# One diffusion layer with mixer and two FFNs: the beginning of the first FFN, the modulation passes beside the mixer and the joint to the second FFN reordered

## Chip, cores and metric

The kernel runs on one core of a Trainium2 chip. The metric is the device time of one launch in microseconds, the median of several runs. Five engines work beside each other, each through its own queue in order: TensorE (PE; its weight loads are shown as PEld), VectorE (DVE), ScalarE (ACT), GpSimd (POOL) and SyncE (SP), which here issues most DMAs.

## The reference

One layer of a diffusion backbone in fp32, batch 1, 256 latent tokens x and 256 context tokens ctx, width D = 2048:

```python
mod_l = (silu(c) @ w_mod + b_mod).reshape(9, D)        # shift, scale, gate of three sub-layers; mod_c likewise
def half_step_ffn(x, mod, i, g, w_up, w_down):
    h = rms_norm(x, g) * (1 + mod[i + 1]) + mod[i]
    a, b = split(h @ w_up, 2)
    return x + 0.5 * mod[i + 2] * ((silu(a) * b) @ w_down)
xl, xc = half_step_ffn(x, mod_l, 0, ...), half_step_ffn(ctx, mod_c, 0, ...)
# mixer: one projection w_in of both sequences; 8 heads of GQA with RoPE over context and latents,
# 8 heads of a bidirectional mLSTM (depthwise convolution of 5 taps and SiLU on its q and k); then w_out
xl = xl + mod_l[5] * mixer(xl, xc)
xl = half_step_ffn(xl, mod_l, 6, ...)
return rms_norm(xl, g_final)
```

`w_mod` alone is 2048 x 18432 numbers, 151 MB. It is read while other work runs.

## The kernel before

**Precision.** Every operand of a large product is split into a high and a low part in fp32r: `split` (L110) lets ScalarE copy a loaded weight to `hi` (L118) and VectorE subtract to get `lo` (L119). A product is three matmuls into the same PSUM bank, `mm3` (L138 to L142): high by high, one mixed product, the other mixed product. Operands named `hhi` and `hlo` are those of the normalised, scaled and shifted tokens.

**Order of the work.** Instructions are written in program order and a scheduler may move them, except where `tc.keep_in_program_order` pins them. `Pinned` (L70) wraps an engine so that every instruction issued through it is pinned; in the first stage VectorE and TensorE are wrapped (L84), ScalarE isn't. Their instructions all appear as L78 in the trace. Where work of two kinds is to run side by side, Python generators are advanced in turn: `steps` runs one forward some steps, `weave` advances a second one after each step of a first, `drain` runs one to its end.

**The beginning of FFN1** (L449 to L604). SP loads the conditions cc, the four token tiles xs (context 0 and 1, latents 0 and 1, 1 MB each, L510), the small vectors vecs (L511), then units of 1 MB of w_mod, tile `mraw`, into four buffers (L530). `diagonal` (L465) multiplies the conditions with an identity on VectorE, and `spread` (L473) broadcasts them over the 128 partitions by eight fp32 matmuls, copied out to cB by VectorE (context) and ScalarE (latents). `x_tile` (L483) takes the squares of a token tile (ScalarE, L153; half of the last tile's on VectorE), its factor, and scales all its columns. The 16 column groups of 128 are then taken in `BLOCKS` (L36): (0,1), (1,2), then seven of two. For a block, `mod_sums` (L533) multiplies the condition with modulation units on TensorE (`tr<-mraw,cP`), one unit of a two-group block goes to VectorE instead (two passes of 128x2048 over `mraw` and cB, "still", L579), `mod_turned` transposes the rows, the tokens are transposed (`x_turned`, `to_hT`), `affine_split` (L377) applies scale and shift and splits into hhi and hlo, and `products` (L403) multiplies with six groups of w_up1, which it loads as strided pieces (L415). The products of a block are stepped between the modulation units of the next one.

**FFN1** (to L1104) keeps TensorE busy with sums of weights that DMAs accumulate; the change doesn't touch it.

**The mixer** (L1135 to L1718) runs its projections in turn. Beside them, `Beside` (L264) computes modulation rows for the second FFN: 96 passes of 128x1024 on VectorE (`mod_half`, L198, with the pair `sr`, `early` or `late` as its buffer), each over 512 KB of w_mod loaded a few passes ahead into the tiles listed at L1165 (after pass 50 three of them end, after pass `N_MIXER` = 80 two more, so that only sr0 is left until three "late" tiles come at L1632). A list of points (pass, step) at L1167 says before which step of the mixer a pass may be issued; steps are advanced by `next(beside["part"])`, at each loaded weight tile. The mLSTM's queries come from the loop at L1412: for each head four columns of matmuls, a convolution on VectorE (L1287), SiLU on ScalarE (L1420), and mqT (L1422); `latents` (L1345), stepped inside that loop, issues the scores (L1355) of a finished head. Attention (softmax at L1536 to L1559) is followed by `out_proj` (L1656): for four column blocks first the groups (2, 0, 3) of w_out, then, in a second loop (L1710), the last group (1,), with the residual.

**The joint to FFN2** (L1699 to L1764). The residual is transposed (`x2_transposed`), the rest of `beside` drained (L1720), the norm's factor computed and broadcast (`rr`, L1727, rB, L1729). Then the pool of FFN2 opens, `scaled` (L1742) applies the scale, and for four quarters q `products` runs on w_up2, with `scaled` of the next quarter woven in and the exact form `h2` (L1751) after it. The fourth group of the first up-projection is done at L1794 to L1805 (`sab`), and `token_forms` (L1840) begins the sums of tokens with `difference` (L1850) for the rest of FFN2.

Of the kernel before, what the change touches and what calls it, by code (L numbers as in the profile page):

```python
# [32 lines left out]

PACE2 = 70 / 73

# [14 lines left out]
def tile_layer(ctx: ExitStack, tc: tile.TileContext, I: dict, out: bass.AP):  # L50
# [33 lines left out]
    vector, tensor = [nc.vector], [nc.tensor]  # L84
# [25 lines left out]
    def split(raw, n=2048):  # L110
# [3 lines left out]
        for h in range(2):  # L114
            hi = wp.tile([P, 1024], F32R, tag="hi", name="hi", bufs=4)[:, :half]
            lo = wp.tile([P, 1024], F32R, tag="lo", name="lo", bufs=4)[:, :half]
            src = raw[:, h * half : (h + 1) * half]
            nc.scalar.activation(hi, src, AF.Copy)  # L118
            vector[0].tensor_tensor(lo, src, hi.bitcast(F32), op=ALU.subtract)  # L119
            parts.append((hi, lo))  # L120
# [30 lines left out]
    def sumsq(dst, x, n=512):  # L151
        junk = sm.tile([P, 512], BF16, tag="junk", name="junk", bufs=1)
        nc.scalar.activation(junk[:, :n], x, AF.Square, accum_out=dst)  # L153
# [223 lines left out]
    def affine_split(src, n, pairs, hh, hl):  # L377

        h = scratch[-1].tile([P, 2, 256], F32, tag="h", name="h", bufs=2)
        for kk, (k, s) in enumerate(pairs):  # L380
            sc, sh = SC[:, n, s, k : k + 1], SH[:, n, s, k : k + 1]
            nc.scalar.activation(hh[:, kk, :], src[:, kk, :], AF.Identity, scale=sc, bias=sh)
            if kk:
                vector[0].tensor_scalar(h[:, kk, :], src[:, kk, :], sc, sh, op0=ALU.mult, op1=ALU.add)
            else:
                nc.scalar.activation(h[:, kk, :], src[:, kk, :], AF.Identity, scale=sc, bias=sh)
# [16 lines left out]
    def products(wup, pre, k0, k1, hhi, hlo, early=False):  # L403
# [7 lines left out]
        def load(u0):  # L411
            nu = min(most, 2 * NPRE - u0)
            raw = raw_tile(n * nu)
            tc.keep_in_program_order(
                nc.sync.dma_start(  # L415
                    raw.rearrange("p (u c) -> p u c", u=nu),
                    wup[u0 // 2 : (u0 + nu) // 2, :, :, k0 * P : k1 * P].rearrange("f a p c -> p (f a) c"),
                )
            )
            return raw, nu  # L420

        ahead = load(0)
        if early:
            wt = split(ahead[0], n * ahead[1])
        yield
        for u0 in range(0, 2 * NPRE, most):
            raw, nu = ahead
            if u0 or not early:
                wt = split(raw, n * nu)
            if u0 + most < 2 * NPRE:  # L430
                ahead = load(u0 + most)
            for u in range(nu):
                b = pre[(u0 + u) // 2][u % 2]
                for k in range(k0, k1):
                    w = slice(u * n + (k - k0) * P, u * n + (k - k0 + 1) * P)
                    mm3(b, *wt(w), hhi[:, k, :], hlo[:, k, :], k == 0, k == KT - 1)
# [13 lines left out]
    with pool(name="st", bufs=1) as st:  # L450
# [12 lines left out]
        junk = st.tile([P, 1024], BF16, name="junkv")  # L463

        def diagonal(s):  # L465
            m = raw_tile()[:32]
            m3 = m.rearrange("p (k c) -> p k c", k=KT)
            vector[0].tensor_tensor(
                m3, cc.unsqueeze(1).to_broadcast([32, KT, P]), ident[:32, s * KT : (s + 1) * KT].unsqueeze(2).to_broadcast([32, KT, P]), op=ALU.mult
            )  # L470
            return m

        def spread(s, m):  # L473
            for q in range(4):
                b = pre[q // 2][q % 2]
                w = slice(q * CB, (q + 1) * CB)
                tensor[0].matmul(b, ones[:32, :], m[:, w], start=True, stop=True)
                if s:
                    nc.scalar.activation(cB[:, s, w], b, AF.Copy)
                else:  # L480
                    vector[0].tensor_copy(cB[:, s, w], b)

        def x_tile(s, t, shared=False):  # L483

            x = xs0[s, t]
            ss4 = sm.tile([P, 4], F32, tag="ss4", name="ss4", bufs=4)
            for cb in range(NCB):
                if not (shared and cb % 2):
                    sumsq(ss4[:, cb : cb + 1], x[:, cb * CB : (cb + 1) * CB])
                else:  # L490
                    xc = x[:, cb * CB : (cb + 1) * CB]
                    vector[0].scalar_tensor_tensor(junk[:, :CB], xc, 1.0, xc, op0=ALU.mult, op1=ALU.mult, accum_out=ss4[:, cb : cb + 1])
            s1 = sm.tile([P, 1], F32, tag="s1", name="s1")
            vector[0].tensor_reduce(s1, ss4, axis=AX.X, op=ALU.add)
            r = rsqrt_mean(s1, D)
            for c in (slice(0, 256), slice(256, D)):
                vector[0].tensor_scalar(x[:, c], x[:, c], r, None, op0=ALU.mult)
# [9 lines left out]
        for s in (CTX, LAT):  # L507
            for t in range(2):
                x = xs0[s, t] = st.tile([P, D], F32, name=f"xs{s}{t}")
                tc.keep_in_program_order(nc.sync.dma_start(x, xsrc[s][t * P : (t + 1) * P, :]))  # L510
        tc.keep_in_program_order(nc.sync.dma_start(vecs, I["vecs"]))  # L511
        diagonals = [diagonal(s) for s in (CTX, LAT)]
        spread(CTX, diagonals[0])
        x_tile(CTX, 0)
        x_turned(0, CTX, 0)
        spread(LAT, diagonals[1])
        for s, t in ((CTX, 1), (LAT, 0), (LAT, 1)):
            x_tile(s, t, s == LAT and t == 1)
            x_turned(0, s, t)

# [4 lines left out]
        prods = iter(())  # L525
        unit = iter(range(32))

        def mod_unit():
            raw = st.tile([P, 2048], F32, tag="mraw", name="mraw", bufs=4)
# [3 lines left out]
        def mod_sums(i, k0, k1, last=iter(())):  # L533
# [16 lines left out]
            nc.scalar.activation(row, b, AF.Copy)  # L550
# [18 lines left out]
        for k0, k1 in BLOCKS:  # L569
            kk = slice(k0, k1)  # L570
            following = products(I["w_up1"], pre, k0, k1, hhi, hlo, k0 == 0)
            if k1 - k0 == 2:
                raw = mod_unit()
            for i in range(2):
                for _ in mod_sums(i, k0 if i else k1 - 1, k1, following if i else iter(())):
                    steps(prods, 3 - (k1 - k0))
                if k0 == 0:
                    mod_turned()
# [10 lines left out]
            if k1 - k0 == 1:  # L589
                tb = tbank() if k0 else first_tb  # L590
                if k0:
                    for s in (CTX, LAT):
                        for t in range(2):
                            x_turned(k0, s, t, tb)
# [5 lines left out]
            prods = following  # L600
            if k1 == KT:
# [43 lines left out]
    with pool(name="f1u", bufs=1) as f1u:  # L645
# [26 lines left out]
        for f in range(NPRE, FB):  # L672
            pab = []
            for ab in range(2):
                wt = load_split(I["w_up1"][f, ab])
# [459 lines left out]
    with ExitStack() as mx:  # L1135
        m1 = mx.enter_context(pool(name="m1", bufs=2))
# [22 lines left out]
        mm = mx.enter_context(pool(name="mm", bufs=1))  # L1159
        mm2cm = pool(name="mm2", bufs=1)  # L1160
        mm2 = mm2cm.__enter__()
        N_EARLY, N_MIXER = 50, 80
# [4 lines left out]
        mods = Beside(mm, 5, 8, tiles, ((6, 12), (N_EARLY, 54), (62, 90), (72, 126), (N_MIXER, 162), (96, 176)))  # L1167
# [244 lines left out]
        for h in range(NH):  # L1412
            b = bank()[:, :T]
            for n, _ in enumerate(channels("w_mq", h, T, b)):
                if (h, n) in ((0, 3), (1, 2)):
                    steps(st)
                if n % 2:
                    steps(lat)
# [279 lines left out]

        def x2_transposed(cb):  # L1699
            for k0 in (4 * cb, 4 * cb + 2):  # L1700
                tb = tbank()
                for kk in range(2):
                    for t in range(2):
                        k = k0 + kk
                        nc.tensor.transpose(tb[:, kk * 256 + t * P : kk * 256 + (t + 1) * P], x2[t][:, k * P : (k + 1) * P], ident)
                nc.scalar.activation(x2T[:, k0 : k0 + 2, :], tb.rearrange("p (k c) -> p k c", k=2), AF.Copy)
                yield

        xT = iter(())
        for cb in range(NCB):  # L1710
# [501 lines left out]
```

## Time and profile before

| | us |
|---|---|
| median of 3 runs | 2664.96 |
| lowest, highest | 2663.31, 2666.14 |
| profiled execution | 2667.12 |
| its span in the trace | 2665.4 |
| mean granted TensorE clock | 0.995 |

The profile is one execution, recorded instruction by instruction. Its page gives the busy time of each engine; its views give busy time by stretches (with the granted TensorE clock, 1.00 being full speed), groups of instructions by line, operation and tile, the waits of an engine by what ended them, and a timeline. A row of the timeline has start, duration, engine, line, operation, output and inputs, shape and count, and in brackets how long the engine sat idle before it and what released it. Lines are those of the kernel before; a helper's line (L78, L118, L119, L198) stands for all its callers.

### The profile page before, as it was taken

Reading aid. Unit: us, or ns where it says so; the run is one execution under the profiler, and the core shown is the slowest. Engines: PE = TensorE matmul, PEld = TensorE weight load, DVE = VectorE, ACT = ScalarE, POOL = GpSimd, SP = SyncE. Lnnn points to the kernel's source line nnn. Section 1 sums busy time; section 2 is a strip of 40 time slices with the busy share of each in tenths; the row PEclk is TensorE's granted clock in tenths of the full one; section 3 lists DMA queues with packets and bytes.
Section 4 is the critical chain, followed back from the end, with each engine's and each line's share of the span. In section 5 each row is a group of like instructions: output and inputs, shape, how many; then the busy total and the mean of one; then the engine's idle time right before and its main releaser. Section 6 shows DMA issues by size and latency. Waiting matters only on the chain. (4 is left out here: it accounts for less than half of the span.)

```text
span 2665.4 us, 33742 instructions
## 1 busy us (share of the span) xinstructions
PE 2609.3 (98%) x12718; PEld 2160.6 (81%) x12718; DVE 2118.4 (79%) x2838; ACT 1367.3 (51%) x1748; POOL 211.1 (8%) x271
## 2 busy tenths in 40 slices
PE   8999999999999999999999999998999999999998
PEld 4688887888888878888879889876898888888886
DVE  5797878878888788888886878688698777777867
ACT  4354444544444555444454347454476655555554
POOL 0000001100000100010111000120000000000001
PEclk9999999999999999999999999999999999999999
DMA  9979999999999988889986865567579898989975
GB/s 345 353 211 270 265 277 267 259 275 278 261 282 264 273 229 237 223 207 233 228 236 221 308 226 201 174 221 254 193 253 292 285 291 290 290 274 283 279 228 170
DMA packets 135027, 679.97 MB, mean 255 GB/s; under 512 B 14152, under 2 KB 23624, under 8 KB 73552
## 3 DMA queue, kind: packets, MB, share of 16 engines
q1 hardware_dynamic: 107504, 500.59, 51.1%
q0 software_dynamic: 27360, 177.22, 34.0%
q8 instruction: 100, 1.64, 0.2%
q14 instruction: 63, 0.52, 0.1%
HBM read 659.87 MB, written 17.89 MB: 254 GB/s over the span
## 5 line engine op out<-in xcount | busy, mean ns | idle before, releaser
L118 ACT ACTIVATE hi<-raw 128x1024 fp32r<-128x1024 f32 (+3 forms) x542 | 560.5, 1038 | 613.7 <-PE mm L142 467.6
L119 DVE TENSOR_TENSOR lo<-raw,hi 128x1024 fp32r<-128x1024 f32 (+1 forms) x524 | 630.5, 1209 | 277.1 <-ACT hi L118 259.2
L118 ACT ACTIVATE hi<-chain 128x1024 fp32r<-128x1024 f32 x320 | 337.8, 1059 | 262.4 <-PE mm L142 133.0
L119 DVE TENSOR_TENSOR lo<-chain,hi 128x1024 fp32r<-128x1024 f32 x320 | 387.1, 1222 | 93.6 <-ACT hi L118 91.0
L140 PE MATMUL mm<-hi,hhi 128*128 128x512 f32 (+3 forms) x1024 | 394.6, 386 | 6.9 <-DVE c L747 6.9
L142 PE MATMUL mm<-hi,hlo 128*128 128x512 f32 (+3 forms) x1024 | 387.6, 379 | 0.0
L141 PE MATMUL mm<-lo,hhi 128*128 128x512 f32 (+3 forms) x1024 | 387.4, 378 | 0.1
L198 DVE SCALAR_TENSOR_TENSOR junk<-sraw,cBh 128x1024 fp8e5<-128x1024 f32 x192 | 234.4, 1221 | 29.9 <-DMA sraw<-in_w_mt 27.6
L140 PEld LDWEIGHTS mm<-hi,hhi 128*128 128x128 f32 x1024 | 192.7, 188 | 39.4 <-ACT hi L118 8.6
L142 PEld LDWEIGHTS mm<-hi,hlo 128*128 128x128 f32 x1024 | 192.7, 188 | 33.6
L141 PEld LDWEIGHTS mm<-lo,hhi 128*128 128x128 f32 x1024 | 193.0, 188 | 31.1 <-DVE lo L119 0.3
L142 PE MATMUL mm<-hi,hid2l 128*128 128x512 f32 x352 | 137.6, 391 | 0.0
L140 PE MATMUL mm<-hi,hid2h 128*128 128x512 f32 x352 | 137.4, 390 | 0.0
L141 PE MATMUL mm<-lo,hid2h 128*128 128x512 f32 x352 | 137.3, 390 | 0.0
L140 PE MATMUL mm<-hi,h2hi 128*128 128x512 f32 x320 | 125.2, 391 | 1.5 <-DVE sab L1804 1.5
L141 PE MATMUL mm<-lo,h2hi 128*128 128x512 f32 x320 | 124.8, 390 | 0.0
L142 PE MATMUL mm<-hi,h2lo 128*128 128x512 f32 x320 | 124.8, 390 | 0.0
L644 POOL DMA_DIRECT2D chain<-in_w_up1b x60 | 53.0, 883 | 740.8 <-DVE lo L119 576.2
L140 PE MATMUL mm<-hhi,hi 128*128 128x512 f32 (+1 forms) x288 | 101.9, 354 | 0.0
L142 PE MATMUL mm<-hhi,lo 128*128 128x512 f32 (+1 forms) x288 | 99.5, 345 | 0.0
L141 PE MATMUL mm<-hlo,hi 128*128 128x512 f32 (+1 forms) x288 | 99.2, 345 | 0.0
L198 DVE SCALAR_TENSOR_TENSOR sr<-sr,cBl 128x1024 f32<-128x1024 f32 x66 | 81.0, 1235 | 13.4 <-DMA sr<-in_w_mt 13.2
(477 smaller groups left out, 5515.7 us busy)
## 6 DMA issues: line engine op xcount, KB each, us to landing
raw<-in_w_dn SPq DMA_DIRECT2D x70, 1024.0 KB, 7.3
sraw<-in_w_mt SPq DMA_DIRECT2D x128, 512.0 KB, 7.4
chain<-in_w_up1b POOLq DMA_DIRECT2D x60, 1024.0 KB, 10.9
raw<-in_w_up2b SPq DMA_DIRECT2D x50, 1024.0 KB, 6.9
raw<-in_w_up1b SPq DMA_DIRECT2D x40, 1024.0 KB, 8.5
mraw<-in_w_m SPq DMA_DIRECT2D x32, 1024.0 KB, 7.3
sr<-in_w_mt SPq DMA_DIRECT2D x63, 512.0 KB, 5.4
chain<-in_w_dn POOLq DMA_DIRECT2D x30, 1024.0 KB, 8.4
```

The lines of the kernel that those rows point to most:

```text
L118: nc.scalar.activation(hi, src, AF.Copy)
L119: vector[0].tensor_tensor(lo, src, hi.bitcast(F32), op=ALU.subtract)
L140: tensor[0].matmul(out_ap, sh, mh, start=first, stop=False, skip_group_check=skip)
L141: tensor[0].matmul(out_ap, sh, ml, start=False, stop=False, skip_group_check=skip)
L142: tensor[0].matmul(out_ap, sl, mh, start=False, stop=last, skip_group_check=skip)
L198: ins = nc.vector.scalar_tensor_tensor(junk() if junk else raw, raw, 1.0, cB[s], op0=ALU.mult, op1=ALU.mult, accum_out=mT[:, i, s, kt, h : ...
L644: accum = lambda dst, src: nc.gpsimd.dma_start(dst, src, accum_op=ALU.add)
```

## The change

Nothing of what is computed is left out. Six parts:

1. *Beginning of FFN1.* The conditions are split into fp32r high and low parts and spread by sixteen fp32r matmuls with eight VectorE products of 32x1024 ahead of them; all copies to cB are ScalarE's. vecs and two modulation units are loaded before the token tiles. Block 0's modulation sums and rows are issued before the tokens' scaling. The squares of a tile (two quarters on ScalarE, two on VectorE) are issued before the scaling of the tile ahead of it, only its first 256 columns are scaled at once, and the rest is scaled later (`others`). ScalarE is pinned as well until block (2, 4) is done.
2. *`affine_split`*: ScalarE makes both high parts first, then h of the first half; VectorE h of the second.
3. *`products`*: the weights come from new inputs `w_pre1`, `w_pre2`, laid out so that each load is contiguous. For each unit all matmuls with hhi come first, those with hlo last. A second load may be issued ahead (`both`).
4. *Mixer*: the list of points has 23 entries instead of 6, `N_MIXER` is 85 instead of 80, and one step of `latents`, at (h, n) = (1, 1), is left out of the loop.
5. *Joint to FFN2*: FFN2's pools open before the second loop of `out_proj`, the rest of `beside` is drained before that loop, `scaled` is woven into it, the loads and first step of the first quarter's `products` are issued before the last residual, the last transposes are woven into that quarter, and the factor is computed after it.
6. *Fourth group*: the first subtraction of `difference` is issued after the gate's product.

The core of the diff:

```diff
-        N_EARLY, N_MIXER = 50, 80
-        mods = Beside(mm, 5, 8, tiles, ((6, 12), (N_EARLY, 54), (62, 90), (72, 126), (N_MIXER, 162), (96, 176)))
+        mods = Beside(mm, 5, 8, tiles, PACE)
+PACE = (4, 2), (12, 13), (19, 19), (26, 28), (33, 37), (37, 44), (42, 51), (48, 54), (52, 61), (55, 70), (58, 76), (59, 85), (63, 96)
+PACE += (70, 102), (72, 109), (75, 118), (76, 130), (77, 144), (80, 152), (83, 163), (85, 166), (86, 174), (96, 181)
+        N_EARLY, N_MIXER = 50, 85
...
-            if kk:
-                vector[0].tensor_scalar(h[:, kk, :], src[:, kk, :], sc, sh, op0=ALU.mult, op1=ALU.add)
-            else:
-                nc.scalar.activation(h[:, kk, :], src[:, kk, :], AF.Identity, scale=sc, bias=sh)
+        for kk, (sc, sh) in enumerate(cols):
+            scalar[0].activation(hh[:, kk, :], src[:, kk, :], AF.Identity, scale=sc, bias=sh)
+        scalar[0].activation(h[:, 0, :], src[:, 0, :], AF.Identity, scale=cols[0][0], bias=cols[0][1])
+        vector[0].tensor_scalar(h[:, 1, :], src[:, 1, :], *cols[1], op0=ALU.mult, op1=ALU.add)
...
-                for k in range(k0, k1):
-                    mm3(b, *wt(w), hhi[:, k, :], hlo[:, k, :], k == 0, k == KT - 1)
+                for k, (wh, wl) in ws:
+                    tensor[0].matmul(b, wh, hhi[:, k, :], start=k == 0, stop=False)
+                    tensor[0].matmul(b, wl, hhi[:, k, :], start=False, stop=False)
+                for k, (wh, wl) in ws:
+                    tensor[0].matmul(b, wh, hlo[:, k, :], start=False, stop=k == KT - 1)
...
+        def squares(s, t):
+            ss4 = sm.tile([P, 4], F32, tag="ss4", name="ss4", bufs=4)
+            for cb in range(NCB):
+                xc = xs0[s, t][:, cb * CB : (cb + 1) * CB]
+                if cb >= 2:
+                    vector[0].scalar_tensor_tensor(junk[:, :CB], xc, 1.0, xc, op0=ALU.mult, op1=ALU.mult, accum_out=ss4[:, cb : cb + 1])
+                else:
+                    sumsq(ss4[:, cb : cb + 1], xc)
+            return ss4
...
+        tc.keep_in_program_order(nc.sync.dma_start(vecs, I["vecs"]))
+        ready += [mod_unit(), mod_unit()]
+        for s in (CTX, LAT):
+            for t in range(2):
+                x = xs0[s, t] = st.tile([P, D], F32, name=f"xs{s}{t}")
+                tc.keep_in_program_order(nc.sync.dma_start(x, xsrc[s][t * P : (t + 1) * P, :]))
+        prods = products(1, pre, 0, 1, hhi, hlo, True)
+        scalar[0] = Pinned(nc.scalar)
+        for copy in spread(CTX, diagonals(CTX)):
+            copy()
+        drain(mod_sums(0, 0, 1))
+        drain(mod_sums(1, 0, 1))
+        ms = diagonals(LAT)
+        ss = squares(CTX, 0)
+        mod_turned()
...
+        copies = spread(LAT, ms)
+        r = factor(ss)
+        for n, (s, t) in enumerate(((CTX, 1), (LAT, 0), (LAT, 1))):
+            ss = squares(s, t)
+            if n < 2:
+                copies[2 * n]()
+                copies[2 * n + 1]()
+            first_columns(*divmod(n, 2), r)
+            r = factor(ss)
+        steps(prods)
+        first_columns(LAT, 1, r)
+        x_scaled(0, first_tb)
+        others(2)
...
-                if n % 2:
+                if n % 2 and (h, n) != (1, 1):
                     steps(lat)
...
+        drain(beside["part"])
+        mmcm.__exit__(None, None, None)
+        m1cm.__exit__(None, None, None)
...
             weave(out_proj(cb, (1,), bs), xT)
+            if cb == NCB - 1:
+                pre = [[bank()[:, : T + 2], bank()[:, : T + 2]] for _ in range(NPRE)]
+                prods = products(2, pre, 0, 4, h2hi, h2lo, both=True)
+                steps(prods)
             residual(cb, bs)
...
-            xT = x2_transposed(cb)
-        drain(xT)
-        drain(beside["part"])
+            xT = chain(scaled(cb - 1), x2_transposed(cb)) if cb else x2_transposed(cb)
...
+            if not q:
+                weave(prods, xT)
+                drain(xT)
+                factor()
+            else:
+                weave(prods, scaled(3) if q == 2 else iter(()))
             drain(h2(q))
...
-            nc.vector.tensor_tensor(sa, sa, pab[1], op=ALU.mult)
+            gated = nc.vector.tensor_tensor(sa, sa, pab[1], op=ALU.mult)
...
-                sub(v, h1, h2)
+                with tc.issue_after(gated.ins):
+                    sub(v, h1, h2)
```

222 lines of the change are left out of this document (116 added, 106 removed).

## The prediction

> **What bounds the kernel now.** I read the page first, then the busy time by stretches, then TensorE's waits. The page's first row (engine, busy time, share, instructions):
>
> ```profile
> PE 2609.3 (98%) x12718; PEld 2160.6 (81%) x12718; DVE 2118.4 (79%) x2838; ACT 1367.3 (51%) x1748; POOL 211.1 (8%) x271
> ```
>
> TensorE is busy 2609.3 of 2665.4 us. The change removes no product of weight, so a gain can come only from the 56 us in which TensorE idles, and from stretches in which its clock was halved. Where are they? Busy time by stretches (columns: PE, PEld, DVE, ACT, POOL busy, granted TensorE clock, DMA share, GB/s):
>
> ```profile
> 32.10:40.00 7.90, 7.39 (x52) 5.18 (x53) 1.93 (x8) 1.18 (x4) 0.00 (x0) 1.00 0.94 340
> 40.00:132.20 92.20, 87.98 (x747) 58.97 (x745) 65.78 (x118) 35.16 (x68) 0.00 (x0) 1.00 0.96 355
> ...
> 140.00:500.00 360.00, 356.24 (x1601) 294.32 (x1600) 303.30 (x363) 174.75 (x200) 30.11 (x34) 1.00 0.94 262
> ...
> 1600.00:1620.00 20.00, 16.39 (x105) 15.22 (x104) 14.51 (x29) 11.16 (x20) 0.76 (x2) 0.83 0.52 182
> 1830.00:1870.00 40.00, 32.51 (x148) 24.03 (x147) 36.29 (x69) 16.36 (x28) 1.36 (x2) 0.91 0.68 235
> 1870.00:1910.00 40.00, 40.00 (x197) 33.42 (x196) 27.06 (x40) 17.68 (x23) 0.00 (x0) 1.00 0.50 168
> ```
>
> The FFN itself (140 to 500) and the output projection (1870 to 1910) leave TensorE idle 1% or less. Two stretches of the mixer stand out. In 1600 to 1620 it idles 3.6 us, and the clock of 0.83 costs another 20 x 0.17 = 3.4 us. In 1830 to 1870 it idles 7.5 us, and 0.91 costs 40 x 0.09 = 3.6. What it waited for (us in total, times, longest):
>
> ```profile
> PE mm L1355 <- DVE mqT L1422: 3.6, 1, 3.6
> PE tr L1550 <- DVE pr L1544: 3.6, 1, 3.6
> ...
> PE mm L78 <- DVE hlo L78: 2.6, 4, 0.8
> ...
> PE mm L78 <- DVE lo L78: 2.0, 7, 0.4
> ...
> PE mm L140 <- DVE sab L1804: 1.5, 1, 1.5
> ...
> PE tr L78 <- DMA mraw<-in_w_m: 1.0, 3, 0.4
> ...
> PE tr L1728 <- DVE rr L1727: 0.8, 1, 0.8
> ```
>
> Nearly all these end on VectorE: TensorE is the bound, and its gaps are places where VectorE's order in program brings one small result late. I take the change in four terms.
>
> **1. The beginning.** The first product of FFN1 starts at 32.07 (start, duration, engine, line, operation):
>
> ```profile
> 29.84 1.94 PE L78 MATMUL tr<-mraw,cP 128*32 128x128 f32 x32
> 32.07 0.80 PE L78 MATMUL mm<-hhi,hi 128*128 128x512 f32 x1 [0.29 <-ACT hhi L382]
> ...
> 39.75 0.60 PE L78 MATMUL tr<-ident,xs 128*128 128x128 f32 x4
> ```
>
> Ahead of it lie these (groups of the first 32 us: busy us, mean ns):
>
> ```profile
> L153 ACT ACTIVATE junk<-xs 128x512 bf16<-128x512 f32 x14 | 8.8, 629 | 3.6 <-DMA xs<-in_ctx 3.2
> ...
> L78 DVE TENSOR_TENSOR raw<-cc,ident 32x2048 f32<-32x2048 f32 x2 | 4.5, 2271 | 0.0
> ...
> L479 ACT ACTIVATE cB<-mm 128x512 f32<-128x512 f32 x4 | 2.4, 597 | 3.9 <-PE mm L78 3.9
> ...
> L382 ACT ACTIVATE hhi<-mm,SH,SC 128x256 fp32r<-128x256 f32 x2 | 1.1, 564 | 1.2 <-DVE SC L78 1.2
> ```
>
> and the loads (the bandwidth in 40 slices of the first 30 us, and the token squares, whose first instruction starts when the first 1 MB tile has landed):
>
> ```profile
> GB/s 0 0 21 175 284 426 415 404 426 415 448 404 437 415 459 404 448 393 415 459 368 310 380 395 448 415 437 404 437 297 369 438 437 371 98 0 109 175 437 393
> ...
> L153 ACT ACTIVATE junk<-xs x14: 629/629/630, 6.1 to 15.9; 128x512 bf16<-128x512 f32 x14
> ```
>
> At 426 GB/s, 1 MB takes 2.46 us, so data flow from about 6.1 - 2.5 = 3.6. SP's queue now issues cc, vecs, two modulation units, the four token tiles, the first weights, then modulation again. Two units and vecs push every token tile back by 2 x 2.46 + 0.35 (vecs has 144 KB) = 5.3 us: ctx lands at 11.4 and 13.8, x at 16.3 and 18.7, the first 384 KB of weights at 19.7. In exchange block 0's modulation rows, which came behind the tiles before, are done while x is still landing.
>
> The spread of the conditions becomes eight VectorE products of 32x1024, about half of 2271 ns each, 9.1 us instead of 4.5; it starts near 3.8 and ends near 13, under the loads. Its fp32r matmuls are not in this trace: between the 0.4 us of a 128x512 product here and the fp32 ones that they replace; I take the former, and either end is hidden under the landing of x. ScalarE's queue is now in program order: the squares of x's first tile at 16.3 (two of 0.63 plus 0.12 of read-out, 1.5), two cB copies (1.2), the squares of the second (1.5): 20.5. Sum, rsqrt, 256 columns and the transpose take about 2.2 more with their handovers, the split 2 x 0.56, and one modulation unit of 1.94 stands ahead of the first product in TensorE's order. That gives 25.8; with the weights' splits (0.5 each) in ScalarE's queue in between I take 26.7, **5.4 us earlier**. What is deferred (1792 columns of each tile, 1.15 each by half of the difference of such rows) goes behind the first split, in VectorE's slack (65.78 of 92.20).
>
> Then the pitch of the blocks. The scaling's new order and the products' new order meet here:
>
> ```profile
> 92.00 0.56 ACT L386 ACTIVATE h<-tr,SH,SC 128x256 f32<-128x256 f32 x1
> ...
> 92.44 1.02 ACT L382 ACTIVATE hhi<-tr,SH,SC 128x256 fp32r<-128x256 f32 x2
> ...
> 93.04 0.55 DVE L78 TENSOR_SCALAR h<-tr,SC,SH 128x256 f32<-128x256 f32 x1 [2.65 <-ACT hhi L382]
> ...
> 96.61 0.50 PE L78 MATMUL mm<-hhi,lo 128*128 128x512 f32 x1 [0.27 <-DVE lo L78]
> ```
>
> VectorE's h waited for ScalarE's second hhi; with both hhi first it can start 0.45 earlier, and hlo and lo behind it. But hlo is asked for last now and lo second, one matmul of 0.23 sooner than before, and lo comes behind hlo on VectorE, so the hlo wait of 2.6 does not vanish: it turns into a lo wait. Net 0.22 a block, 1.5 over seven; the mraw waits (1.0) should shrink, since the units are loaded ahead. The relaid weights load in fewer, longer pieces, but no row shows TensorE waiting for them: nothing. Term: 5.4 + 1.5 + 0.3 = **7**, bounds 3.5 (half of the earlier start) and 10 (all waits of the blocks gone).
>
> **2. The first mLSTM scores** wait for mqT:
>
> ```profile
> 1600.90 1.22 DVE L198 SCALAR_TENSOR_TENSOR sr<-sr,cBl 128x1024 f32<-128x1024 f32 x1
> ...
> 1602.05 1.22 DVE L198 SCALAR_TENSOR_TENSOR sr<-sr,cBl 128x1024 f32<-128x1024 f32 x1
> ...
> 1605.89 1.22 DVE L119 TENSOR_TENSOR lo<-raw,hi 128x1024 fp32r<-128x1024 f32 x1 [0.18 <-ACT hi L118]
> ...
> 1608.05 0.29 DVE L1422 TENSOR_SCALAR mqT<-cy 128x256 f32<-128x256 f32 x1 [0.15 <-ACT cy L1420]
> ...
> 1608.49 2.05 PE L1355 MATMUL mm<-mqT,mkT 128*128 128x256 f32 x4 [3.61 <-DVE mqT L1422]
> ```
>
> In the changed order one pass instead of two stands ahead of this convolution on VectorE (1.15 of pitch), and one weight split fewer (1.2). The scores keep their place behind the second column's 48 matmuls (only the second scores move, by 24), so the wait falls by about 2.1 to 1.5, not to nothing. Is 1.5 short enough for the clock? Before, the one idle of 3.61 led to the 0.83. Two other idles (first row the wait, then stretches as above):
>
> ```profile
> 978.16 0.50 PE L141 MATMUL tr<-lo,hidl 128*128 128x512 f32 x1 [1.86 <-DVE lo L119]
> ```
> ```profile
> 979.00:982.40 3.40, 3.40 (x10) 2.63 (x9) 3.11 (x4) 0.17 (x1) 0.00 (x0) 0.50 0.57 195
> 1836.00:1842.00 6.00, 3.79 (x16) 2.49 (x14) 6.00 (x12) 1.12 (x2) 1.36 (x2) 1.00 0.74 283
> ```
>
> After 1.86 us of idle the clock was 0.50 for 3.4 us, while the 2.2 us in 1836 to 1842 left it at 1.00; so 1.5 is near the edge but below both, and I take no loss. The Trainium skill ("TensorE: Matmul & The Clock Gate", Part 1) has the clock halved after an idle window of about 3.4 us; by that rule 1.5 is safe by far, and the trace's 1.86 speaks against relying on it. Term: 2.1 + 3.4 = **5.5**; bounds 2 (clock still lost) and 7.
>
> **3. The end of attention.** VectorE executes the modulation passes in order, and behind the 80th only one buffer is left to load into (line and shape, count, duration min/median/max; then what the passes waited for, 1800 to 1900):
>
> ```profile
> L198 DVE SCALAR_TENSOR_TENSOR sr<-sr,cBl x10: 1215/1224/1226, 1804.1 to 1872.4; 128x1024 f32<-128x1024 f32 x10
> ...
>   DMA sr<-in_w_mt: 6.1, 6
> ```
>
> Six waits for a load, 6.1 us, and passes of 1.22 stand ahead of the splits, the rotary sums and the softmax that TensorE asks for next. With 85 passes on three buffers and the next due at step 174, the order on VectorE shows none between the last attention copies and the first output projection, where seven stood. Seven passes and their waits are some 12 us of VectorE's in front of gaps of 7.5: those of lo and rotary go, of the last softmax's 3.6 I leave up to 1.5, a chain of its own. The passes go into 1770 to 1815 and 1870 to 1910, where VectorE has 27.06 of 40 us to do; their loads move along on SP's queue, and end at step 181 still before the second FFN's scaling. Term: 6 + 3 = **9**; bounds 4 and 10.9.
>
> **4. The joint to FFN2.** The two waits sab 1.5 (two more passes of the token forms issued ahead of it) and rr 0.8 can go: both have other matmuls to hide under once the first forms come behind the gate and the factor behind the first quarter's products. The pools open earlier, and two 1 MB loads are issued on SP ahead of the last residual's stores; the stores have no reader near. Term **1.8**, bounds 0 and 2.3.
>
> **Sum.** 7 + 5.5 + 9 + 1.8 = 23.3, less 1.3 for small waits that passes make elsewhere (I found no stretch with more VectorE work than time; bounds 0 and 6): 22. The profiled execution took 2667.12, 2.16 over the median of 2664.96: 2645 on its scale, **2643** as a median.
>
> **Rivals.** (a) *The passes take their waits along.* The slots' loads are late by up to 1.8 us in the old place, and one VectorE lateness of 2 us at TensorE's side is enough for a halved clock. If the two mixer terms then gain only a third (5 of 14.5) and the rest comes: 2665 - 7 - 5 - 1.8 + 1.3 = 2652.5. For it: VectorE has 36.29 of 40 there; against: the new places have slack. (b) *The beginning is bound by the loads.* If the tiles, 5.3 us later, with ScalarE in order, bring the first product no earlier than 32: 2665 - 1.5 - 5.5 - 9 - 1.8 + 1.3 = 2648.5. For it: the squares were finished at 15.9 + 0.8 and would be at 20.5; against: rows and spread, which came behind them, are then done. (c) *Slower.* Between steps 144 and 166 ten passes run against three buffers; if each pass finds its load late and its lateness reaches TensorE as the worst did (3.6 idle and 3.4 of clock), four such stalls undo 28 us, more than the gain of 22, and five give 2665 - 22 + 35 = 2678. It decides from four on; before, six late loads made one such stall. (d) *Rule of the clock.* If the 1.5 at the scores halves the clock after all, 2643 + 3.4 = 2646; this is inside the forecast's own range.
>
> **Chances.** Forecast with (d), 2636 to 2650: 0.52. (b): 0.15. (a): 0.18. (c): 0.08. Better than 2636: 0.07. The range 2632 to 2657 leaves out (c) and part of the ends. One can tell about 0.2%, 5.3 us, from no change: faster 0.87, within 0.2% 0.05 (the worst of (a)), slower 0.08.
>
> **What would show it.** First product at 25.5 to 28, the block transposes after it at about 33 instead of 39.75, hlo waits gone and lo waits of FFN1 grown to about 3; L1422's wait of 1 to 2 us with clock 1.00 behind it; no load wait of sr on VectorE in 1830 to 1860 of the old scale, and TensorE idle there under 2; sab and rr gone from the waits. A PEclk under 1 in a new place of the mixer, or a first product after 30, would prove the sum wrong.

## The result

| | us, median (range) | runs |
|---|---|---|
| before | 2665.55 (2663.31 to 2667.19) | 4 |
| changed | 2645.54 (2643.48 to 2649.92) | 4 |
| before, a later series | 2665.58 (2662.91 to 2671.26) | 7 |
| changed, the same later series | 2641.37 (2640.60 to 2642.25) | 4 |

The ratio is 0.9928, 95% interval 0.9910 to 0.9945; in the later series 0.9907, 0.9890 to 0.9924. The change makes the kernel 20 to 24 us faster; 22 was forecast.

The changed kernel's lines are 5 higher where they were around 78 to 198 (L78 is L83, L119 is L124, L198 is L203), and 54 or 55 higher in the mixer (L1355 is L1409, L1422 is L1477, L1544 is L1599). Its page, first row, and TensorE's waits over the whole profile (span 2648.2, time 2649.92, the slowest of its four runs):

```profile
PE 2598.3 (98%) x12718; PEld 2154.5 (81%) x12718; DVE 2123.5 (80%) x2854; ACT 1365.9 (52%) x1741; POOL 221.9 (8%) x271
```

```profile
PE mm L83 <- DVE xs L83: 6.6, 4, 1.8
PE mm L83 <- DVE lo L83: 6.4, 8, 1.7
...
PE tr L83 <- DVE SH L83: 1.9, 1, 1.9
...
PE tr L1454 <- DVE kvs L1535: 1.3, 1, 1.3
PE mm L1409 <- DVE mqT L1477: 1.1, 1, 1.1
PE mm L1591 <- DVE qT L1546: 1.0, 1, 1.0
...
PE tr L1454 <- DVE hm L1463: 0.8, 1, 0.8
...
PE tr L1605 <- DVE pr L1599: 0.6, 2, 0.5
PE mm L145 <- DVE sab L1874: 0.6, 1, 0.6
```

Three things are to be seen. The two waits of 3.6 are 1.1 and 0.6 now. The waits for hlo and for mraw are gone, but waits for lo in the beginning have grown from 2.0 to 6.4, and one for SH is new. TensorE's busy time fell by 11 us with the same count of 12718 matmul records: the sixteen of the spread take about 7 us where the fp32 ones took 14.4, and the two stretches of 6.8 us at half clock behind the waits of 3.6 are gone. The stretches that stood out before, at their new times:

```profile
32.20:128.40 96.20, 89.02 (x747) 60.10 (x746) 68.10 (x122) 35.65 (x70) 0.00 (x0) 0.98 0.93 354
1595.00:1615.00 20.00, 18.89 (x146) 18.18 (x145) 18.59 (x38) 15.37 (x25) 2.77 (x2) 1.00 0.56 194
1822.50:1853.60 31.10, 29.73 (x148) 22.07 (x147) 26.64 (x54) 15.32 (x27) 4.44 (x2) 1.00 0.53 188
1853.60:1893.60 40.00, 40.00 (x197) 33.39 (x196) 31.16 (x44) 17.54 (x21) 0.00 (x0) 1.00 0.59 210
```

The third row holds the 148 matmuls that took 40 us before (1830 to 1870): 31.1 us now, at full clock and with 1.4 idle. The first row is the other side: the 747 matmuls of blocks 2 to 8 took 92.2 and take 96.2.

**Where the time came from.** TensorE executes the same matmuls in both kernels, but for those of the spread. The start of one and the same matmul before, less its start after, is the lead at that place; the growth of the lead over a part is that part's gain. At the first matmul of FFN1's fourth column (before, then changed):

```profile
145.75 0.39 PE L140 MATMUL mm<-hhi,hi 128*128 128x512 f32 x1
```
```profile
142.33 0.39 PE L145 MATMUL mm<-hhi,hi 128*128 128x512 f32 x1
```

the lead is 3.4. Taken as the median over many matmuls at each boundary (times of the profile before), for this profile and for that of the changed kernel in the later series (2640.60):

| part | forecast | first profile | later profile |
|---|---|---|---|
| beginning, to 150 | 7 | 3.4 | 5.9 |
| FFN1, not touched, 150 to 1420 | 0 | -0.8 | 5.6 |
| first scores, 1590 to 1620 | 5.5 | 5.8 | 5.8 |
| rest of the mixer to 1810 | -1.3 | 1.7 - 2.6 | 1.7 - 2.2 |
| end of attention, 1830 to 1870 | 9 | 8.9 | 8.9 |
| joint, 1930 to the end | 1.8 | 0.8 | 1.0 |
| sum | 22 | 17.2 | 26.6 |

The two large terms of the mixer repeat to 0.1 us, the loss after them to 0.4. The beginning gave less than forecast, and the untouched FFN1 differs by 6.4 us between two profiles of the same instructions. Both needed experiments.

### The profile page after: what moved, and what is told of

The parts are those of the page before. It is cut to its first block, busy times and chain, and to the rows that moved or that the text cites. A ratio compares the mean times of both kernels' runs of the same rounds, so it can differ in the third digit from the quotient of the medians.

```text
span 2648.2 us, 33739 instructions
## 1 busy us (share of the span) xinstructions
PE 2598.3 (98%) x12718; PEld 2154.5 (81%) x12718; DVE 2123.5 (80%) x2854; ACT 1365.9 (52%) x1741; POOL 221.9 (8%) x271
## 5 line engine op out<-in xcount | busy, mean ns | idle before, releaser
L123 ACT ACTIVATE hi<-raw 128x1024 fp32r<-128x1024 f32 (+2 forms) x538 | 558.1, 1042 | 600.5 <-PE mm L147 454.0
L124 DVE TENSOR_TENSOR lo<-raw,hi 128x1024 fp32r<-128x1024 f32 (+1 forms) x524 | 630.6, 1210 | 254.0 <-ACT hi L123 229.6
L124 DVE TENSOR_TENSOR lo<-chain,hi 128x1024 fp32r<-128x1024 f32 x320 | 387.1, 1221 | 99.3 <-ACT hi L123 96.8
L203 DVE SCALAR_TENSOR_TENSOR junk<-sraw,cBh 128x1024 fp8e5<-128x1024 f32 x192 | 234.2, 1220 | 23.7 <-DMA sraw<-in_w_mt 21.4
L203 DVE SCALAR_TENSOR_TENSOR sr<-sr,cBl 128x1024 f32<-128x1024 f32 x65 | 78.9, 1225 | 8.7 <-DMA sr<-in_w_mt 8.6
```

Of the source, the lines that this page charges most:

```text
L123: scalar[0].activation(hi, src, AF.Copy)
L203: ins = nc.vector.scalar_tensor_tensor(junk() if junk else raw, raw, 1.0, cB[s], op0=ALU.mult, op1=ALU.mult, accum_out=mT[:, i, s, kt, h : ...
```

## Experiments

Two questions: what ate the beginning's lead, and which edit of the mixer did what. Runs without an interval are single profiles; there the start of the fourth column (142.33 in the changed kernel) is the measure, not the time.

**1. The deferred scalings on ScalarE.** In block (2, 4):

```diff
-                    others(2)
+                    for _ in range(2):
+                        x, r = rest.pop(0)
+                        scalar[0].activation(x, x, AF.Copy, scale=r)
```

> The changed kernel, with block (2, 4)'s two deferred scalings of 1792 columns on ScalarE (which sat idle from 37.9 to 39.9 and 40.3 to 44.3 there) and not on VectorE. Theory: the 2.2 us of these scalings stood on VectorE ahead of the two passes over mraw and made TensorE wait 1.85 us for SH at 43.6, and 1.46 us for lo at 47.4. Then the SH wait goes, the lo wait falls to about 0.5 as in the later blocks, and the first matmul of the fourth column (142.33 in the changed kernel, 145.75 before) starts at 139.3 to 140. Rival: the deferred columns are under cover and TensorE waits for the loads or the modulation rows there; then the waits come back under other names and the fourth column starts at 142 to 142.5.

The rows of the changed kernel to which this answers (TensorE, then VectorE):

```profile
32.24 0.60 PE L83 MATMUL tr<-ident,xs 128*128 128x128 f32 x4
...
43.59 1.09 PE L83 MATMUL tr<-ident,xs 128*128 128x128 f32 x8 [1.85 <-DVE SH L83]
```
```profile
36.52 2.21 DVE L83 TENSOR_SCALAR xs<-xs,rstd 128x1792 f32<-128x1792 f32 x2
38.64 2.28 DVE L83 SCALAR_TENSOR_TENSOR junkv<-mraw,cB 128x2048 fp8e5<-128x2048 f32 x1
...
40.97 2.29 DVE L83 SCALAR_TENSOR_TENSOR junkv<-mraw,cB 128x2048 fp8e5<-128x2048 f32 x1
```

Measured: fourth column at 138.94, no wait for SH, but a wait of 0.8 for a load of mraw that was not there, and the lo wait of 1.45 in that block unchanged. So the 1.85 came from VectorE's order, as the theory had it, while the lo wait does not come from these scalings: it ends 5.7 to 5.8 us after the transposes of its own block in both kernels, whenever these come. Set beside the second profile of the changed kernel (139.90, with the same 10.2 us of half clock in its beginning, and waits of 1.3 for SH and 0.5 for mraw) the edit is worth 1.0, less than the 2.3 to 3.0 of the theory.

**2. The products in the old order.**

```diff
-                for k, (wh, wl) in ws:
-                    tensor[0].matmul(b, wh, hhi[:, k, :], start=k == 0, stop=False)
-                    tensor[0].matmul(b, wl, hhi[:, k, :], start=False, stop=False)
-                for k, (wh, wl) in ws:
-                    tensor[0].matmul(b, wh, hlo[:, k, :], start=False, stop=k == KT - 1)
+                for k in range(k0, k1):
+                    w = slice(u * n + (k - k0) * P, u * n + (k - k0 + 1) * P)
+                    mm3(b, *wt(w), hhi[:, k, :], hlo[:, k, :], k == 0, k == KT - 1)
```

> The changed kernel, with the products' matmuls in the order of before (high by hhi, high by hlo, low by hhi). Theory: VectorE makes hlo ahead of lo, so asking for lo second costs one matmul of 0.23 us in each of eight blocks; with the old order lo waits fall from 6.4 by 0.23 x 8 = 1.8 and the fourth column starts at 140.4 to 141 instead of 142.33. Rival: the hlo waits (2.6 us before) come back on top, and it starts at 142.3 or later.

Measured (waits of the first 145 us of this kernel):

```profile
PE mm L83 <- DVE hlo L83: 2.1, 4, 0.8
PE tr L83 <- DVE SH L83: 2.0, 1, 2.0
PE mm L83 <- DVE lo L83: 2.0, 7, 0.4
```

lo 2.0 and hlo 2.1 in place of lo 6.4, fourth column at 139.65. Beside a run of the changed beginning with the same clock (run 7 below, 141.36, 13.7 us of half clock each) that is 1.7, the 0.23 us a block of the theory. The rival is out: the sum of the two waits fell by 2.3. Asking for the later of two operands first only names the wait differently, and gives away the matmul that could have run.

**3 and 4. The scaling's order.** Two attempts to have VectorE's h earlier:

```diff
         for kk, (sc, sh) in enumerate(cols):
             scalar[0].activation(hh[:, kk, :], src[:, kk, :], AF.Identity, scale=sc, bias=sh)
-        scalar[0].activation(h[:, 0, :], src[:, 0, :], AF.Identity, scale=cols[0][0], bias=cols[0][1])
         vector[0].tensor_scalar(h[:, 1, :], src[:, 1, :], *cols[1], op0=ALU.mult, op1=ALU.add)
+        scalar[0].activation(h[:, 0, :], src[:, 0, :], AF.Identity, scale=cols[0][0], bias=cols[0][1])
```

and ScalarE's h first of all:

```diff
+        scalar[0].activation(h[:, 0, :], src[:, 0, :], AF.Identity, scale=cols[0][0], bias=cols[0][1])
+        vector[0].tensor_scalar(h[:, 1, :], src[:, 1, :], *cols[1], op0=ALU.mult, op1=ALU.add)
         for kk, (sc, sh) in enumerate(cols):
             scalar[0].activation(hh[:, kk, :], src[:, kk, :], AF.Identity, scale=sc, bias=sh)
-        scalar[0].activation(h[:, 0, :], src[:, 0, :], AF.Identity, scale=cols[0][0], bias=cols[0][1])
-        vector[0].tensor_scalar(h[:, 1, :], src[:, 1, :], *cols[1], op0=ALU.mult, op1=ALU.add)
```

> The changed kernel, with VectorE's h of the second half written ahead of ScalarE's h of the first half in the program. Theory: VectorE's h waited (16.0 us, 6 times) for ScalarE's h only because that came before it; now it waits for the second hhi alone, 0.45 us earlier, and hlo and lo follow by up to 0.45 in each of eight blocks: lo waits 6.4 down to 3 to 4.5, the fourth column at 139.5 to 141. Rival: hlo needs ScalarE's h anyway, which is as late as before, so VectorE waits at hlo instead and the fourth column stays at 142.3.

> The changed kernel with the scaling in another order: ScalarE h of the first half, VectorE h of the second right behind it, then ScalarE's two hhi. Theory: two engines write two halves of one tile, and the second writer waits for the first; with ScalarE's h first VectorE's wait ends after one ScalarE instruction and not after three, and hlo and lo come 0.4 to 0.6 us earlier in every block. The lo waits of 6.4 fall to 2 to 3.5 and the fourth column starts at 137.5 to 140. Rival: hlo waits for the second hhi, now the last of the three, and lo comes as late as before: fourth column at 142 to 143.

Both missed, and in the wrong direction: the fourth column at 151.37 and 150.19, lo waits 11.8 and 11.1. VectorE and ScalarE in one block of the second attempt:

```profile
91.09 0.54 DVE L83 TENSOR_SCALAR h<-tr,SC,SH 128x256 f32<-128x256 f32 x1 [1.80 <-ACT h L386]
92.72 0.69 DVE L83 TENSOR_TENSOR hlo<-h,hhi 128x512 fp32r<-128x512 f32 x1 [1.09 <-ACT hhi L389]
```
```profile
90.49 1.02 ACT L386 ACTIVATE h<-tr,SH,SC 128x256 f32<-128x256 f32 x2 [3.34 <-PE tr L83]
91.67 1.02 ACT L389 ACTIVATE hhi<-tr,SH,SC 128x256 fp32r<-128x256 f32 x2 [0.16 <-DVE h L83]
93.90 1.02 ACT L389 ACTIVATE hhi<-tr,SH,SC 128x256 fp32r<-128x256 f32 x2 [1.21 <-DVE h L83]
```

hhi doesn't touch the tile h, and yet ScalarE waits for VectorE's h. What they share is the transposed bank that both read. (They share SC and SH too, but those reads do overlap: in run 3 ScalarE's four hhi, of both sequences, run from 76.58 to 78.51, and VectorE's h of the first at 77.64.) So the theory of the shared output falls, and this remains as the reading that fits all these rows: in this program the reads of one PSUM tile by two engines are kept in program order. Whichever comes second waits, and the order in both the kernel before and the changed one, with VectorE's read last, is the one with a single handover. The reordering of `affine_split` should therefore have brought nothing, since h starts after three ScalarE instructions in both; no run takes it back by itself.

**5. The mixer as before, in the changed kernel** (old list, limit 80, the step kept).

> The changed kernel with the mixer's list of points, the limit of 80 and the latents' step as before: the first FFN's beginning and the joint alone. Theory (the mixer terms gave 14 of the 17 us between the two profiles: 1.8 at 1500 to 1540, 5.8 at the first scores, 8.9 at the end of attention, less 2.5 in 1700 to 1820): 2645.5 + 14 = 2657 to 2662, waits for mqT and pr of 3 us or more back. Rival: the beginning and the joint carry more of it and the mixer's waits were moved only: 2650 to 2654.

Measured: 2657.24 (2654.21 to 2662.51); ratio to before 0.9981, 0.9967 to 0.9995, 6.1 us under the median of before beside it. Waits for mqT and pr of 3.6 each are back; the rival is out. In its profile the beginning leads by 5.7 and the joint adds 1.7.

**6. The mixer alone, in the kernel before.**

```diff
+PACE = (4, 2), (12, 13), (19, 19), ...
-        N_EARLY, N_MIXER = 50, 80
+        N_EARLY, N_MIXER = 50, 85
...
-                if n % 2:
+                if n % 2 and (h, n) != (1, 1):
```

> The kernel before with the mixer's part alone (list of points, limit of 85, the latents' step). Theory: it gains the mixer terms: 2665.5 - 14 = 2649 to 2654, waits for mqT and pr under 1.5. Rival: it needs the shifted joint (the rest of the passes is drained ahead of the second loop of the output projection) and gains half, 2656 to 2660.

Measured: 2648.95 (2648.44 to 2652.03); ratio 0.9946, 0.9931 to 0.9961: 14.4 us under the median of before beside it. Its waits for mqT and pr are 1.1 and 0.4; from 1420 to 1930 its lead grows by 14.2. The mixer's part is 14 of the 20 to 24, and it doesn't need the joint. Together with the 6.1 of run 5 it makes 20.5.

**7. Only the end of the list as before.**

```diff
-PACE += (70, 102), (72, 109), (75, 118), (76, 130), (77, 144), (80, 152), (83, 163), (85, 166), (86, 174), (96, 181)
+PACE += (70, 102), (72, 109), (75, 118), (76, 130), (77, 144), (80, 162), (96, 176)
...
-        N_EARLY, N_MIXER = 50, 85
+        N_EARLY, N_MIXER = 50, 80
```

> The changed kernel with only the last points of the list as before, from (77, 144) straight to (80, 162) and (96, 176), and the limit of 80: passes 81 to 96 stand at the end of attention again. Theory: the end of attention's 8.9 us are lost and nothing else: 2653 to 2656, waits of sr for its loads of 4 to 6 us, TensorE's wait for pr of 2 to 3.6 with a halved clock. Rival: the gain there came from the passes before (75 to 80 earlier, at steps 118 to 152): the time stays within 3 us of 2645.5.

Measured: 2652.58 (2650.85 to 2654.37). The end of attention adds 1.2 to its lead instead of 8.9, and the mixer ahead of it is as in the changed kernel (scores 5.8). Its stretch around the end of attention, and what VectorE's passes waited for between 1790 and 1860:

```profile
1820.00:1860.00 40.00, 34.36 (x157) 25.14 (x156) 36.43 (x71) 15.38 (x28) 1.36 (x2) 0.91 0.63 226
```
```profile
  DMA sr<-in_w_mt: 3.0, 4
```

Clock 0.91 and VectorE at 36.4 of 40 again. The passes waited half as long for loads as before (3.0 us in four waits against 6.1 in six), less than the 4 to 6 expected, and the loss is nearly the same: the passes' own 1.2 us each in front of the softmax cost more than their late loads.

**8 and 9. The step and the list, each alone, in the kernel before.**

> The kernel before with one edit of the mixer alone: the step of the latents at (1, 1) left out. Theory: the first scores keep their place and their wait of 3.6 us for mqT, since only VectorE's order with one pass fewer shortens it: wait 3 to 4 us with the halved clock behind it, time 2662 to 2668. Rival: the left-out step is what took the wait away: wait under 1.5, no halved clock there, time near 2659.

> The kernel before with the mixer's list of points and the limit of 85 alone, the latents' step kept. Theory after the run with the step alone: the list of points acts at the end of attention only and the left-out step at the first scores only. So the wait for mqT is 3 us or more as before, TensorE's waits for pr, lo and sq in 1800 to 1860 fall under 2 together, and no wait for kvs appears near 1715. Time 2654 to 2660. Rival: the spacing of the passes in steps 54 to 61 takes a pass away from ahead of mqT as well, so that wait falls under 2: near 2650.

The step alone: wait for mqT 1.1, 5.8 us of lead at the scores, time 2660.24. My theory fell and its rival held. VectorE ahead of mqT in this run:

```profile
1593.79 1.22 DVE L198 SCALAR_TENSOR_TENSOR sr<-sr,cBl 128x1024 f32<-128x1024 f32 x1
...
1596.09 1.23 DVE L119 TENSOR_TENSOR lo<-raw,hi 128x1024 fp32r<-128x1024 f32 x1
...
1599.47 0.29 DVE L1422 TENSOR_SCALAR mqT<-cy 128x256 f32<-128x256 f32 x1 [1.04 <-ACT cy L1420]
```

One pass and one split where two of each stood, with the old list of points. TensorE issues the first scores behind the same products of the projection. What the left-out step moved is VectorE's order, and also four small products of the state (L1304): they stood behind the scores (1610.33 in the profile before) and stand ahead of them now:

```profile
1596.42 1.10 PE L1304 MATMUL mm<-vw,kn 128*128 128x260 f32 x4
...
1599.82 1.13 PE L1355 MATMUL mm<-mqT,mkT 128*128 128x256 f32 x4 [1.11 <-DVE mqT L1422]
```

The next product starts 0.75 us after the first of the four, so 0.75 of the 2.5 us by which the wait fell are TensorE's own order, and the rest VectorE's. What is left of the wait stands behind ScalarE's SiLU, for which VectorE waits 1.04 us ahead of mqT.

The list alone: wait for mqT 2.6, 3.3 us of lead at the scores (its 2.6 did not halve the clock), time 2653.07. So the theory that the list acts at the end of attention only fell as well. The two overlap at the scores. Away from there the step alone loses 3.1 between 1650 and 1810 and another 2.9 at the end of attention, the list alone loses 2.3 in the former; the changed kernel 2.6. Which of VectorE's instructions makes that new loss (waits for kvs 1.3, hm 0.8, qT 1.0) isn't settled: the wait for kvs appears with the step and not with the list alone.

**10 and 11. Combinations.** The first holds edits 1, 2 and 4, the second 1 and 2.

> The changed kernel with three edits together: ScalarE's h ahead of the two hhi, block (2, 4)'s deferred scalings on ScalarE, and the products' matmuls in the old order. Theory: the lo waits are gone but for two of the first blocks, fourth column at 136.5 to 138.5, that is 4 to 6 us ahead of the changed kernel: 2640 to 2643. Rival: the loads of mraw bind once VectorE does not (the first of these edits already showed 0.8 of such a wait): fourth column at 139 to 140, 2643 to 2645.

> The changed kernel with two edits: block (2, 4)'s deferred scalings on ScalarE, and the products' matmuls in the old order; the scaling's order as in the changed kernel. Theory: each of the two gave 1.1 to 1.7 us by itself where the clock was in the same state, and they act on different waits (SH, and lo in each block), so together the fourth column starts at 136 to 138.5 and the time is 2 to 4 us under the changed kernel's in the same call. Rival: the gains seen in single profiles were the clock's; then the two kernels agree within 1 us.

With edit 4: 2652.74 (2649.76 to 2654.22), fourth column at 147.13, a loss, as edit 4 by itself, and not for the loads that the rival named (there is no wait for mraw). Without it: 2640.31 (2639.55 to 2644.08), fourth column at 137.53, beside 2641.37 for the changed kernel in the same series; the ratio to before is 0.9905 (0.9889 to 0.9921) against 0.9907 (0.9890 to 0.9924). The beginning is 2.4 us shorter in the profile, but the times can't be told apart.

**12. The changed kernel again.**

> The changed kernel itself once more, as the measure for the run beside it and as a second profile of the same instructions. Theory: the first FFN behind its beginning is untouched, and the 3.1 us that the first profile lost there against the profile before (3.4 ahead at 150 us, 0.3 at 800 to 950) are waits of 2 us that halve the clock in one run and not in another; so in this profile the half clock lies in other places of 150 to 1400 and the lead at 1400 differs by 1 to 4 us. Rival: the loss is a property of the changed kernel; then the half clock comes at 459 and 698 again.

Measured: lead 5.9 at 150 and 11.4 at 1420 (3.4 and 2.6 in the first profile, a larger difference than expected), no half clock between 150 and 1400. The same wait in the first and in this profile, and the clock behind it:

```profile
457.65 0.47 PE L145 MATMUL mm<-hi,hhi 128*128 128x512 f32 x1 [2.28 <-DVE c L799]
...
459.00:462.40 3.40, 3.40 (x12) 2.64 (x11) 3.40 (x5) 0.00 (x0) 0.00 (x0) 0.51 1.02 417
698.00:701.40 3.40, 3.40 (x10) 2.53 (x9) 3.40 (x6) 0.00 (x0) 0.00 (x0) 0.50 0.99 410
```
```profile
454.94 0.47 PE L145 MATMUL mm<-hi,hhi 128*128 128x512 f32 x1 [1.85 <-DVE c L799]
...
459.00:462.40 3.40, 3.40 (x17) 2.78 (x16) 2.35 (x3) 2.14 (x3) 0.00 (x0) 1.00 1.04 361
```

FFN1 is the same instructions in both. Two of its waits were 2.3 and 2.0 in the first profile and halved the clock for 3.4 us each, 1.7 lost each time; here they were 1.9 and 1.2 and did not. The rival is out. That is 3.4 of the 6.4 us between the two; most of the rest is the waits themselves, which differ from run to run (for c, L799: 7.0 in the first, 4.7 here).

## Why the prediction was right, and where it was not

**The sum** came out (22 forecast; 20 and 24 measured), and not because every term did. The parts that the change touches give 18.0 and 21.0 us in the two profiles of the table; what FFN1 adds, -0.8 and 5.6, belongs to no term. That the medians lie on both sides of 22 is in part luck. The joint's term is read from the lead alone: no run takes the joint back by itself, nor the relaid weights.

**The end of attention (9)** was right in place and size: 8.9 twice, and run 7 takes it away with the list's end alone. That the six late loads do much of the harm was half right: with half the waiting for loads (run 7) the loss was nearly whole.

**The first scores (5.5)** were right in size: 5.8, a wait of 1.1 and a full clock. The count of VectorE's instructions (one pass and one split fewer) was the right way to see it, though 0.75 of the 2.5 us by which the wait fell came from products that moved ahead of the scores (run 8), which the forecast did not have. The prediction left open which edit did this and spoke of the left-out step as moving only the second scores; run 8 shows that this step does it by itself.

**The beginning (7)** was the mis-sized term: 3.4 and 5.9. Its first half was better than forecast: first product at 25.62 instead of 26.7, block transposes at 32.24, a lead of 7.5 there. (The clock of 1.00 that the view gives for 32.10 to 40.00 before is no record: the record begins at 36.9 there, and a product of 128x512 takes 0.63 us ahead of that and 0.39 to 0.40 after it.) From there to the fourth column TensorE idles 8.9 us (8.8 in the second profile) where it idled 5.4. Two steps of the forecast failed there. "Goes behind the first split, in VectorE's slack": the slack was an average over 92 us, and in block (2, 4) the 2.2 us stood ahead of the two long passes; TensorE waited 1.85 there (run 1). And "with both hhi first it can start 0.45 earlier": it can't, since VectorE's read of the transposed bank waits for all three of ScalarE's (runs 3 and 4). So nothing paid for asking for lo one matmul sooner, and in place of the forecast gain of 1.5 stands a loss of 1.7 (run 2). The forecast that hlo waits turn into lo waits was right; that they would be 3 was not (6.4). The first profile lost 1.7 more to the clock, which the forecast had at nothing and the second profile doesn't have; this is most of the difference between 3.4 and 5.9:

```profile
49.45:52.87 3.42, 3.42 (x17) 1.99 (x21) 3.38 (x4) 1.58 (x2) 0.00 (x0) 0.50 1.01 428
```

Rival (b), a first product no earlier than 32 for the loads, did not come: the first product was early, and the lead was lost afterwards.

**The joint (1.8)** gave 0.8 to 1.7: the wait of rr is gone, sab's fell from 1.5 to 0.6. **The small losses (1.3)** were 2.2 to 2.6, between 1650 and 1810, set against 1.7 gained near 1520. Of these, 1.2 and 1.1 stand in run 5 and in the step alone (run 8) too, which have the old list; only the remaining 0.5 to 0.6 can be the new list's doing.

**The rivals.** (a) and (c), passes that take their waits along, did not come: the changed kernel's passes waited 1.6 us for a load, once, between 1750 and 1920. (d), a halved clock behind the scores' remaining wait, did not come either: 1.00 in 1595 to 1615. But the clock's edge matters, in the part that nobody changed: a wait near 2 us costs 1.7 more in one run and not in the next. The forecast had 0 there, and its range was wide enough by the other terms only.

**The rule of the Trainium skill** that the prediction weighed ("TensorE: Matmul & The Clock Gate", Part 1) also says that the window is free-running. The traces agree: all stretches of half clock inside the work last 3.41 us or a multiple, and in each profile they lie on one grid of 3.413 us from beginning to end (in the profile before they begin at 979.01, 1607.07 and 1852.83, 184 and 72 steps apart). They don't agree with taking some 3.4 us of idle as the limit: 1.86, 2.0 and 2.28 were enough here. The prediction's second example was misread: 2.2 us is all the idle time in 1836 to 1842, and its one wait, 1.92 us from 1837.91 to 1839.83, is cut by a line of the grid at 1839.17 into 1.26 and 0.66. That the wait of 1.1 at the scores left the clock alone was right all the same.

## What to carry to other kernels

Count the instructions that stand ahead of one late result on the engine that makes it; here one pass and one split moved behind it, with four small products moved ahead of the wait, were worth 5.8 us, clock included, and this count held where guesses on causes did not. Slack is local: read an engine's order between two deadlines, not its busy share over the stretch. And before blaming an edit for a few microseconds in a part that it doesn't touch, profile the same kernel twice.

## What the runs showed of the hardware

Whether a wait of TensorE halves the clock depended on how much idle time fell into one step of the grid of 3.413 us. In the 14 profiles, from 150 to 2600 us and counting steps at full clock, all 14 steps with 2.0 us of idle or more were followed by a step at half clock, 6 of the 10 with 1.8 to 2.0, and none of some 10,000 with less. A longer wait passes where a line of the grid cuts it: the 2.6 of the list alone (run 9) lies across 1601.86, with 1.47 and 1.11 us of idle on its two sides, and the clock stays full. Two steps of the profile before, then two of run 9:

```profile
975.60:979.01 3.41, 1.55 (x8) 0.96 (x7) 3.41 (x4) 3.41 (x4) 0.00 (x0) 1.00 0.11 43
979.01:982.43 3.42, 3.42 (x10) 2.65 (x9) 3.10 (x4) 0.16 (x1) 0.00 (x0) 0.50 0.58 201
```
```profile
1598.44:1601.86 3.42, 1.95 (x17) 1.74 (x15) 2.82 (x5) 2.04 (x5) 0.00 (x0) 1.00 0.93 375
1601.86:1605.27 3.41, 2.30 (x13) 2.11 (x14) 3.22 (x8) 0.55 (x2) 0.00 (x0) 1.00 0.54 153
```

The same wait can so be halved or not by where the grid lies in that run. Near 1.9 us even this does not decide: the wait of 1.86 at 978 that halved the clock in the profile before stands at the same place, with the same length and within one step, in the first profile of the changed kernel, and the clock behind it is full:

```profile
977.87 0.50 PE L146 MATMUL tr<-lo,hidl 128*128 128x512 f32 x1 [1.86 <-DVE lo L124]
...
979.00:982.40 3.40, 3.40 (x17) 2.79 (x16) 3.40 (x5) 0.28 (x1) 0.00 (x0) 1.00 0.70 231
```

Through such stretches, and through waits that vary from run to run, a part of 1270 us of the same instructions differed by 6.4 us. And a scaling of 1792 columns in place costs VectorE 1.1 us and ScalarE 1.74 (3.48 for two, in run 1).
